# Thirty-two spare bytes between the chunks of two operand tiles

## The chip, the cores and the metric

The kernel is one program on one core of a Trainium2 chip. The metric is device time in microseconds (us) of that core. Its engines are TensorE (PE in the profile; PEld is its loading of weights), VectorE (DVE), ScalarE (ACT), GpSimd (POOL) and SyncE (SP), which issues most of the DMAs.

## The reference

Two layers of a transformer over 256 image tokens and 256 context tokens, D = 1024, all in float32. Layer 0 mixes tokens by retention (4 heads), layer 1 by attention in a neighbourhood window (32 heads). Around each mixer and each MLP stand a modulation by six vectors made from a conditioning input, a gated residual and a layer norm:

```
mod = (silu_c @ ada_w[i] + ada_b[i])[:, None, :]
sh1, sc1, g1, sh2, sc2, g2 = jnp.split(mod, 6, axis=-1)
h = x * (1.0 + sc1) + sh1
y, yc = mixer(h, hc, ...)                 # projections of h and hc, then scores, then w_o
x = layer_norm(DN_ALPHA * x + g1 * y, ln_g[i, 0], ln_b[i, 0])
h = x * (1.0 + sc2) + sh2
x = layer_norm(DN_ALPHA * x + g2 * (square(relu(h @ w1)) @ w2), ln_g[i, 1], ln_b[i, 1])
```

The context stream `hc`/`ctx` goes through the same steps in layer 0. The output is x, 256 x 1024.

## The kernel before

**Products.** Every float32 operand of a large product is split into a high and a low half (float32r tiles `hi` and `lo`; for a weight: DMA to `raw`, an ACT cast to `hi`, a DVE subtraction to `lo`). `mm3` then issues three matmuls into one PSUM bank: high x high, high x low, low x high. Each matmul first loads its stationary operand (128 columns) and then streams the moving one (512 or 256 columns); PE loads the next weights while it streams.

**The tiles of the change.** The modulated activations are kept transposed, channels on partitions, in `hTh` (high half) and `hTl` (low half): eight chunks of 128 channels, chunk k holding 512 tokens, 2048 bytes in each partition. `hs(k, a, b)` returns columns a to b of chunk k of both. They are the moving operand of the products named pq (queries and keys of retention), p (MLP hidden, from banks p1) and pn (queries and keys of layer 1), and the stationary operand of pv and pg (values and gates), pnv (values of layer 1) and p1t (four small MLP pieces). The products named p that read `hid` (second MLP matrix), pw, po, pS, pnw do not touch them.

**Where tiles lie.** Pools put tiles one behind the other. Small tiles are rounded up to 64 bytes (`LINE`, 16 floats), and every tile that a large product reads has a size that is a multiple of 512 bytes. In the built program hTh starts at byte 40,896 of each partition and hTl at 57,280, and these, all `hi`, `lo`, `raw`, `hid`, `qkh` and the rest start at 448 modulo 512. So the distance between the streamed operand of any split product and the weights that are loaded beside it is 0 modulo 512 bytes. A chunk's own start is a multiple of 64 bytes. The exceptions among PE's operands are small: `onecol` is read from byte 132 or 128 modulo 512, `cT` from 0, 128, 256 or 384, `natv` from 448, 64, 192 or 320, the identity in `cst` from 192.

**The row tile.** The modulation vectors of later stages are made in the background (`bg_stream`, L491): eight `rawa` loads are weighed and added (on DVE into `acc` or `strips`, or by matmuls), `fold_rows` sums them over partitions on PE (pada<-acc,onecol), `ada_row` (L414) adds the bias on DVE into a tile `row`, and `ada_columns` (L421) turns it by four small matmuls on PE (pada<-cst,row); parts that are gates go to DRAM instead (grow<-row). Before, `row` has a buffer of its own in the pool `smp` (one buffer of 1024 bytes), so a new row waits until the last one's readers are done. `scr` (L164) hands out one of eight buffers of 2048 bytes that all short-lived results share (`aff`, `r`, `s`, `acc`, `on`, `sg`, ...).

**What sets the order.** Code is recorded in program order and a scheduler places each engine's instructions by its own costs, except where an engine's `on` is set (then it keeps program order) and on SP. The order on each engine is fixed in the built program; engines wait for each other by semaphores. PE takes its instructions in that order, so a matmul that waits holds all behind it.

Of the kernel before, what the change touches and what calls it, by code (L numbers as in the profile page):

```python
# [10 lines left out]
F32 = mybir.dt.float32  # L11
F32R = mybir.dt.float32r
# [5 lines left out]
P = 128  # L18
D = 1024
KC = D // P  # L20
NT = 512
# [83 lines left out]
def kernel(  # L105
# [30 lines left out]
    smp = ec(tc.tile_pool(name="smp", bufs=4))  # L136
    cpool = ec(tc.tile_pool(name="cpool", bufs=1))
# [14 lines left out]
    def nm(s):  # L152
        uid[0] += 1
        return f"{s}_{uid[0]}"
# [8 lines left out]
    def scr(s, dt=F32):  # L163
        return scp.tile([P, 512], dt, tag="scr", name=nm(s))  # L164
# [248 lines left out]

    def ada_row(pr, brow, nb, p0=0, p1=P, row=None):  # L414
        if row is None:
            row = smp.tile([P, 256], F32, tag="row", name=nm("row"), bufs=1)
        dve.tensor_add(out=row[p0:p1, :nb], in0=pr[p0:p1, 0:nb], in1=brow[p0:p1, :nb])
        return row

# [50 lines left out]
    def bg_stream():  # L470
# [13 lines left out]
        for step, (l, w, part, offs, n) in enumerate(plan):  # L484
# [8 lines left out]
            if on_pe(l, w, part):  # L493
                if n == 0:
                    pr = bank("pada")
                ada_mm(pr, n, 256, lambda j: raw[:, j // 2, (j % 2) * 256 : (j % 2 + 1) * 256])
                if n == KC - 1:
                    row = ada_row(pr, brow, 256)
            elif l == 0:
                for kk in range(2):  # L500
                    for t in range(nt):
                        weigh(spare(t), raw[:, kk, :], t, 2 * (n % 4) + kk, n % 4 == 0 and kk == 0)
                if n % 4 == 3:
                    yield
                    s = n // 4
                    pr = bank("pada")
                    fold_rows(pr, (2 * s, 2 * s + 1), nt, spare)
                    row = ada_row(pr, brow, 256, 64 * s, 64 * s + 64, row)
            else:
                if n == 0:  # L510
                    acc = slot(S_VL, [P, 2, D], F32, "acc")
                for t in range(nt):

                    dve.on = n == 0 and (w, part) == (0, 0)
                    weigh(acc[:, t], raw[:].rearrange("p a n -> p (a n)"), t, n, n == 0)
                    dve.on = False
                if n == KC - 1:
                    pr = bank("pada")
                    fold_rows(pr, range(4), nt, lambda t: acc[:, t])
                    row = ada_row(pr, brow, 256)  # L520
# [32 lines left out]
        return G  # L553


    hTh = cpool.tile([P, KC, NT], F32R, tag="hTh", name="hTh")
    hTl = cpool.tile([P, KC, NT], F32R, tag="hTl", name="hTl")

    def hs(k, a, b):
        return hTh[:, k, a:b], hTl[:, k, a:b]  # L560
# [188 lines left out]
    def quarter_rows(i, raws):  # L749
        pr = bank("pada")  # L750
        for kh in range(2):
            quarter_ada(pr, raws, kh)
        return pr, ada_row(pr, brows[:, i], P)
# [33 lines left out]
    pr, row = quarter_rows(0, raws)  # L787
# [7 lines left out]
    for i in range(4):  # L795
        k = 2 * i
        quarter_q(k, 0, wq)
        if i < 3:
            pr, row = quarter_rows(i + 1, raws)
# [1073 lines left out]
```

## Time and profile before

| | |
|---|---|
| three runs | 1233.33, 1235.42, 1235.53 us; median 1235.42 |
| the profiled execution | 1232.81 us, of which the span of instructions is 1231.0 us |
| granted TensorE clock, mean | 0.994 of 2.4 GHz |
| PE busy | 1196.5 us, 97% |
| DVE, ACT, POOL busy | 809.1 (66%), 478.7 (39%), 170.7 us (14%) |
| HBM traffic | 158 GB/s over the span |

A matmul's time in the profile runs from its start to its modelled end, and neighbours overlap; what it costs a busy PE is the distance from one start to the next, called the pace below. A busy DVE costs nothing while PE has work; a chain of waits tells where it does.

### The profile page before, as it was taken

What the parts mean: (1) busy time and instruction counts of PE and PEld (TensorE: products, weight loads), DVE (VectorE), ACT (ScalarE), POOL (GpSimd) and SP (SyncE); (2) the same over time, 40 slices, a digit from 0 to 9 for tenths busy, and PEclk for the clock granted to TensorE, in tenths of its full rate; (3) what the DMA queues carried; (4) which work ended last, traced back from release to release, by engine and by line L of the source; (5) the groups of instructions that cost most, each with busy time, mean ns of one, the idle gap of its engine ahead of it and who ended that gap; (6) DMA issues with size and microseconds to landing.
All of it is one profiled execution on the core that took longest, in us unless ns stands there. A gap on an engine that the chain in (4) does not pass through costs nothing.

```text
span 1231.0 us, 17933 instructions
## 1 busy us (share of the span) xinstructions
PE 1196.5 (97%) x7069; PEld 999.1 (81%) x7069; DVE 809.1 (66%) x1256; ACT 478.7 (39%) x796; POOL 170.7 (14%) x202
## 2 busy tenths in 40 slices
PE   6999999999999999999999999999999989999996
PEld 4777888888888888888888888788787867999885
DVE  2597857777586476667666664467575678776445
ACT  2462232223223255442113342156465666565331
POOL 2004401410330140000120000131111100000002
PEclk9999999999999999999999999999999999999998
DMA  9765443375543224326656556336245543565650
GB/s 307 229 209 194 143 130 107 120 247 127 144 154 107 80 67 140 110 87 207 198 170 203 194 190 207 125 92 182 86 138 161 184 138 120 185 208 187 225 189 35
DMA packets 140660, 194.53 MB, mean 158 GB/s; under 512 B 22456, under 2 KB 84384, under 8 KB 140576
## 3 DMA queue, kind: packets, MB, share of 16 engines
q1 hardware_dynamic: 135872, 181.39, 46.2%
q0 software_dynamic: 3264, 9.46, 3.0%
q10 hardware_dynamic: 1440, 2.55, 0.6%
q8 instruction: 55, 0.90, 0.3%
q14 instruction: 29, 0.24, 0.1%
HBM read 188.53 MB, written 5.75 MB: 158 GB/s over the span
## 4 chain that ended last, share of the span: by engine, by line
PE 85%; DVE 6%; ACT 4%; DMA 2%; issue 1%; POOL 1%; DVEq 0%; SPq 0%; ACTq 0%; POOLq 0%
PE p L84 41%; PE pv L84 7%; PE pq L84 7%; PE pw L84 6%; PE pg L84 6%; PE pn L84 4%; PE pnv L84 3%; PE pada L84 2%; PE po L84 2%; ACT s L84 2%; DVE lo L84 1%; DMA rawa<-in_ada_w_dram 1%; PE ppt L84 1%; PE pS L84 1%; ACT hi L84 1%
## 5 line engine op out<-in xcount | busy, mean ns | idle before, releaser
L84 DVE TENSOR_TENSOR lo<-raw,hi 128x1024 fp32r<-128x1024 f32 (+1 forms) x227 | 278.1, 1234 | 159.4 <-ACT hi L84 158.2
L84 ACT CAST hi<-raw 128x1024 fp32r<-128x1024 f32 (+1 forms) x227 | 233.8, 1039 | 354.6 <-PE p L84 185.5
L84 PE MATMUL p<-hi,hid 128*128 128x512 f32 (+1 forms) x832 | 242.6, 374 | 0.0
L84 PEld LDWEIGHTS p<-hi,hid 128*128 128x128 f32 x832 | 152.3, 188 | 28.7 <-issue 1.2
L84 PE MATMUL p<-hTh,lo 128*128 128x256 f32 (+1 forms) x512 | 169.8, 332 | 0.8 <-DVE lo L84 0.8
L84 PE MATMUL p<-hTh,hi 128*128 128x256 f32 (+1 forms) x512 | 170.1, 333 | 0.0
L84 PE MATMUL p<-hTl,hi 128*128 128x256 f32 (+1 forms) x512 | 169.5, 331 | 0.0
L84 PE MATMUL p<-lo,hid 128*128 128x512 f32 (+1 forms) x416 | 155.5, 374 | 0.0
L84 POOL TENSOR_TENSOR R<-R,acc 128x512 f32<-128x512 f32 x40 | 65.9, 1656 | 299.0 <-DVE acc L84 298.8
L84 PEld LDWEIGHTS p<-hTh,lo 128*128 128x128 f32 x512 | 98.1, 192 | 9.8 <-DVE lo L84 1.0
L84 PEld LDWEIGHTS p<-hTh,hi 128*128 128x128 f32 x512 | 98.1, 192 | 9.5 <-issue 0.8
L84 PEld LDWEIGHTS p<-hTl,hi 128*128 128x128 f32 x512 | 98.1, 192 | 8.7
L84 DVE SCALAR_TENSOR_TENSOR acc<-rawa,scol,acc 128x1024 f32<-128x1024 f32 x49 | 62.1, 1282 | 46.7 <-DMA rawa<-in_ada_w_dram 46.6
L84 PEld LDWEIGHTS p<-lo,hid 128*128 128x128 f32 x416 | 78.4, 189 | 13.5
L84 DVE SCALAR_TENSOR_TENSOR strips<-rawa,scol,strips 128x512 f32<-128x512 f32 x84 | 69.9, 885 | 4.9 <-DMA rawa<-in_ada_w_dram 4.9
L84 ACT CAST hid<-r 128x256 fp32r<-128x256 f32 (+1 forms) x64 | 32.0, 500 | 83.5 <-DVE r L84 83.5
L84 POOL TENSOR_SCALAR rstd<-mv 128x1 f32<-128x1 f32 x28 | 9.8, 350 | 364.7 <-DVE mv L84 364.7
L84 ACT ACTIVATE s<-s,mn 128x512 f32<-128x512 f32 x64 | 45.5, 712 | 32.3 <-DVE mn L84 32.3
L84 DVE TENSOR_TENSOR hid<-r,hid 128x256 fp32r<-128x256 f32 (+1 forms) x64 | 34.6, 541 | 29.8 <-ACT hid L84 29.6
L84 PE MATMUL pq<-hTh,hi 128*128 128x512 f32 x128 | 49.9, 393 | 2.0 <-ACT hTh L84 2.0
L84 PE MATMUL pw<-hi,oh 128*128 128x512 f32 x128 | 51.3, 401 | 0.0
L84 PE MATMUL pg<-hi,hTh 128*128 128x512 f32 x128 | 51.0, 398 | 0.0
(192 smaller groups left out, 2249.5 us busy)
## 6 DMA issues: line engine op xcount, KB each, us to landing
raw<-in_mlp_w_dram SPq DMA_DIRECT2D x128, 512.0 KB
rawa<-in_ada_w_dram SPq DMA_DIRECT2D x80, 512.0 KB
raw<-in_ret_w_in_dram SPq DMA_DIRECT2D x46, 512.0 KB
raw<-in_nat_w_in_dram SPq DMA_DIRECT2D x24, 512.0 KB
rawq<-in_ada_w_dram SPq DMA_DIRECT2D x16, 512.0 KB
raw<-in_ret_w_o_dram SPq DMA_DIRECT2D x16, 512.0 KB
bias<-rpb_rows POOLq DMA_DIRECT2D x16, 256.0 KB, 4.1
raw<-in_nat_w_o_dram SPq DMA_DIRECT2D x8, 512.0 KB
```

The source lines that it names most:

```text
L84: r = f(*args, **kwargs)
```

## The change

`hTh` and `hTl` are allocated with 520 columns a chunk instead of 512 and used through a view of the first 512. Chunk k of hTh now starts at 448 + 32k modulo 512 and, since a tile is now 16,640 bytes, chunk k of hTl at 192 + 32k: sixteen different distances (0, 32, ... 480 modulo 512) to the weights, some 140 to 270 products on each. Chunks with odd k start at an odd multiple of 32 bytes. The two tiles grow by 512 bytes in sum; to make room `row` gives up its own buffer and is taken from the shared `scr` buffers. All other large tiles move down by 512 or 1024 bytes and keep 448 modulo 512. The number of instructions on every engine stays the same.

```
     def ada_row(pr, brow, nb, p0=0, p1=P, row=None):
         if row is None:
-            row = smp.tile([P, 256], F32, tag="row", name=nm("row"), bufs=1)
+            row = scr("row")[:, :256]
         dve.tensor_add(out=row[p0:p1, :nb], in0=pr[p0:p1, 0:nb], in1=brow[p0:p1, :nb])
         return row
...
-    hTh = cpool.tile([P, KC, NT], F32R, tag="hTh", name="hTh")
-    hTl = cpool.tile([P, KC, NT], F32R, tag="hTl", name="hTl")
+    hTh = cpool.tile([P, KC, NT + 8], F32R, tag="hTh", name="hTh")[:, :, :NT]
+    hTl = cpool.tile([P, KC, NT + 8], F32R, tag="hTl", name="hTl")[:, :, :NT]
```

Since `row` comes from other buffers, the scheduler places a few instructions of DVE, POOL, SP and PE otherwise, all in the background modulation beside the second half of layer 0's MLP. Two places matter below. The first is DVE at the start of the last quarter of the second MLP matrix (775 us in the trace before), where acc_6189 to acc_6198 empty four finished banks, the BN_STATS begin a layer norm, and row_6183 is a row whose turning PE waits for. Before:

```order
L84 TENSOR_TENSOR lo_6148<-raw_6145,hi_6147 128x1024
L84 TENSOR_TENSOR acc_6189<-p_935_5900,G_4624 128x512
L84 TENSOR_TENSOR acc_6192<-p_936_5901,G_4624 128x512
L84 BN_STATS st_6340<-R_110 128x6
L84 TENSOR_TENSOR acc_6195<-p_937_5902,G_4624 128x512
L84 BN_STATS st_6342<-R_110 128x6
L84 BN_STATS st_6344<-R_111 128x6
L84 TENSOR_TENSOR row_6183<-pada_6178,brow_5942 128x256
L84 TENSOR_TENSOR acc_6198<-p_938_5903,G_4624 128x512
```

There the row stands behind three of the four emptyings and three BN_STATS. On the same engine, now:

```order
L84 TENSOR_TENSOR lo_6148<-raw_6145,hi_6147 128x1024
L84 TENSOR_TENSOR row_6183<-pada_6178,brow_5942 128x256
L84 TENSOR_TENSOR acc_6189<-p_935_5900,G_4624 128x512
L84 TENSOR_SCALAR mod_109<-pada_6178 128x8 x2
L84 TENSOR_TENSOR acc_6192<-p_936_5901,G_4624 128x512
L84 TENSOR_TENSOR acc_6195<-p_937_5902,G_4624 128x512
```

The row is now the first of them, and the emptyings follow it. At two earlier places (595 and 640 us) row_4922 and row_5229 move ahead of four emptyings in the same way.

The second place is the step before it (730 us), on DVE: acc_5945 is the first weighing of the next background step. Before:

```order
L84 TENSOR_TENSOR lo_5907<-raw_5904,hi_5906 128x1024
L84 TENSOR_TENSOR row_5894<-pada_5889,brow_5644 128x256
L84 TENSOR_TENSOR lo_5913<-raw_5910,hi_5912 128x1024
L84 SCALAR_TENSOR_TENSOR r_5878<-p_922_5812,r_5878 128x512
L84 TENSOR_SCALAR mod_109<-pada_5889 128x8 x2
L84 TENSOR_SCALAR acc_5945<-rawa_5886,scol 128x1024
```

Here the row follows a weight's low half directly. Now:

```order
L84 TENSOR_TENSOR lo_5907<-raw_5904,hi_5906 128x1024
L84 TENSOR_SCALAR acc_5945<-rawa_5886,scol 128x1024
L84 TENSOR_TENSOR row_5894<-pada_5889,brow_5644 128x256
L84 SCALAR_TENSOR_TENSOR r_5878<-p_922_5812,r_5878 128x512
L84 TENSOR_SCALAR mod_109<-pada_5889 128x8 x2
L84 TENSOR_TENSOR lo_5913<-raw_5910,hi_5912 128x1024
```

The weighing has come in front of the row; on PE the row's turning, which stood behind three products of bank p_935, now stands behind six.

## Rows read from the trace of the kernel before

**Rows 1.** The page: busy time by engine; the chain that ended last, by engine.
```profile
PE 1196.5 (97%) x7069; PEld 999.1 (81%) x7069; DVE 809.1 (66%) x1256; ACT 478.7 (39%) x796; POOL 170.7 (14%) x202
...
PE 85%; DVE 6%; ACT 4%; DMA 2%; issue 1%; POOL 1%; DVEq 0%; SPq 0%; ACTq 0%; POOLq 0%
```

**Rows 2.** The chain in order of time: start us, us, what, in 140 to 215.
```profile
143.51 21.76 PE pq L84 x96
165.27 21.76 PE pv L84 x96
...
203.72 8.16 PE po L84 x36
```

**Rows 3.** Timeline of PE: first and last narrow product of one run of 24.
```profile
456.30 0.28 PE L84 MATMUL p<-hTh,hi 128*128 128x256 f32 x1
...
459.05 0.28 PE L84 MATMUL p<-hTh,lo 128*128 128x256 f32 x1
```

**Rows 4.** Windows: stretch; busy us of PE, PEld, DVE, ACT, POOL; granted clock, DMA share.
```profile
143.60:165.20 21.60, 21.60 (x97) 17.91 (x96) 19.09 (x30) 5.97 (x10) 3.94 (x2) 1.00 0.48 152
```

**Rows 5.** Groups by shape: products that read hTh (count | busy us, mean ns).
```profile
L84 PE MATMUL p<-hTh,hi 128*128 128x512 f32 x224 | 87.5, 391 | 0.0
...
L84 PE MATMUL p<-hTh,hi 128*128 128x256 f32 x288 | 82.7, 287 | 0.0
...
L84 PE MATMUL pq<-hTh,hi 128*128 128x512 f32 x128 | 49.9, 393 | 2.0 <-ACT hTh L84 2.0
...
L84 PE MATMUL pn<-hTh,hi 128*128 128x256 f32 x96 | 27.6, 287 | 0.0
...
L84 PE MATMUL pnv<-hi,hTh 128*128 128x512 f32 x64 | 25.8, 402 | 0.0
...
L84 PE MATMUL pn<-hTh,hi 128*128 128x512 f32 x48 | 19.3, 402 | 0.0
...
L84 PE MATMUL p1t<-hi,hTh 128*128 128x256 f32 x32 | 9.2, 288 | 0.0
```

**Rows 6.** Groups by shape: weight loads of 32 columns from small tiles.
```profile
L84 PEld LDWEIGHTS pav<-pt,natv 128*32 128x32 f32 x256 | 6.5, 110 | 1.3 <-issue 1.3
...
L84 PEld LDWEIGHTS pada<-strips,onecol 128*32 128x32 f32 x48 | 2.3, 109 | 3.3 <-issue 2.1
```

**Rows 7.** Timeline: transposes, and products of 32 weight columns.
```profile
898.83 0.82 PE L84 MATMUL ppt<-cst,s 128*128 128x128 f32 x6
...
899.68 1.08 PE L84 MATMUL pav<-pt,natv 128*32 128x128 f32 x32
```

**Rows 8.** Timeline of DVE: around the row of 775.88.
```profile
770.50 1.28 DVE L84 TENSOR_TENSOR acc<-p,G 128x512 f32<-128x512 f32 x2
...
775.27 0.69 DVE L84 BATCH_NORM_STATS2 st<-R 128x6 f32<-128x512 f32 x1 [0.74 <-POOL R L84]
775.88 0.41 DVE L84 TENSOR_TENSOR row<-pada,brow 128x256 f32<-128x256 f32 x1
```

**Rows 9.** Timeline of PE: the same place.
```profile
773.60 0.64 PE L84 MATMUL pada<-acc,onecol 128*32 128x256 f32 x8
...
774.75 0.39 PE L84 MATMUL p<-hi,hid 128*128 128x512 f32 x1
776.34 0.61 PE L84 MATMUL pada<-cst,row 128*128 128x8 f32 x4 [1.20 <-DVE row L84]
```

**Rows 10.** Timeline of DVE: around the row of 729.52.
```profile
729.52 0.42 DVE L84 TENSOR_TENSOR row<-pada,brow 128x256 f32<-128x256 f32 x1 [1.19 <-PE pada L84]
...
731.74 0.75 DVE L84 TENSOR_SCALAR acc<-rawa,scol 128x1024 f32<-128x1024 f32 x1
```

**Rows 11.** Timeline of PE: the same place.
```profile
728.81 0.64 PE L84 MATMUL pada<-acc,onecol 128*32 128x256 f32 x8
...
730.18 0.51 PE L84 MATMUL pada<-cst,row 128*128 128x8 f32 x4
```

**Rows 12.** The tile hTl: one DVE write's ns, min/median/max.
```profile
L84 DVE TENSOR_TENSOR hTl<-aff,hTh x24: 628/684/695, 18.3 to 1043.5; 128x512 fp32r<-128x512 f32 x24
```

## The prediction

> **What bounds the kernel now.** I read the page first: PE is busy 97% of the span, and 85% of the chain that ended last is PE [rows 1]. The other engines have slack; so a change counts where it alters the pace of PE's products or the few places where PE stands still. Second, the chain in order of time, for the pace. In it 96 products pq take 21.76 us, 96 products pv as much, and 36 products po 8.16 us: 226.7 ns each, all three times [rows 2]. pq streams the transposed activations, pv loads them as weights, po touches neither; the pace knows no difference. Third, the timeline of a run of narrow products: 23 starts from 456.30 to 459.05, 119.6 ns each, of 256 columns [rows 3]. The window over the pq piece has a granted clock of 1.00, that is 2.4 GHz [rows 4]. There 512 columns are 213.3 ns and 256 are 106.7 ns: either width pays some 13.3 ns more than its columns (226.7 - 213.3; 119.6 - 106.7 = 12.9).
>
> Of this remainder the change can take or add. The products that it touches, from the groups by shape [rows 5]: p has three forms of 224 wide and 288 narrow, pq three forms of 128, and pv and pg (not shown) the same, pn three of 48 wide and 96 narrow, pnv three of 64, p1t three of 32 narrow. Wide: 672 + 1152 + 144 + 192 = 2160. Narrow: 864 + 288 + 96 = 1248. Together 3408; 2160 x 0.2267 + 1248 x 0.120 = 639 us, 52% of the span. One ns on each is 3.4 us.
>
> **The change, part 1: the chunks.** No instruction is added. What may move is the pace at a distance other than 0 modulo 512, and at an odd multiple of 32 bytes. No split product in this trace runs at such a distance, so the cost is bounded from the nearest rows. Below: the whole remainder is a collision of load and stream and goes at fifteen of the sixteen distances, 3408 x 13.3 ns x 15/16 = -42.5 us. Above: a chunk that starts off a 64-byte boundary costs one 64-byte piece more, 16 columns or 6.7 ns, on the half that are odd: 1704 x 6.7 ns = +11.4 us.
>
> The nearest rows say nothing happens. Loads of 32 columns take 110 ns from `natv` at four residues (448, 64, 192, 320), and 109 ns from `onecol`, of which half start at 132, not even at a multiple of 8 [rows 6]. The 32 products from `natv` follow each other in 1.08 us less the last one's 0.27 us (the length of one), 0.81 us for seven and a half steps of four, 108 ns for four of 128 columns, two at a time: no delay at any of four distances [rows 7]. [...] They show that another distance doesn't hurt; they can't show whether it helps, since their streams are shorter than their loads. I take 0.
>
> [...]
>
> Writes into the chunks: 28 casts on ACT, 24 subtractions on DVE and 4 on POOL. They write 512 columns in one chunk or 128 in each of four, and one on DVE takes 628 to 695 ns over both layouts [rows 12]. No write at an odd 32 bytes is in the trace; with that spread as the price, 28 x 0.067 = 1.9 us if PE waited for every one, and as much less at the other end. I take 0: all but a few lie under products.
>
> **Part 2: the row in shared buffers.** This moves instructions, and one move meets a wait of PE. At 774.75 PE starts the third product after pada<-acc,onecol; at its pace the next would start at 774.98, but it is the turning of the row, and starts at 776.34 [rows 9]. The row was late on DVE: it ran at 775.88, behind emptyings and BN_STATS that themselves waited for POOL [rows 8], though pada had ended at 773.60 + 0.64 = 774.24. Now it follows the subtraction before 770.50 directly; DVE waits for pada, and the row is done at 774.24 + 0.41 = 774.65, 0.33 us before PE asks. So the whole wait goes: 776.34 - 774.98 = **-1.36 us**.
>
> What is late instead: four emptyings, two of which ran at 770.50 and now start at 774.65. They set free four of the eight PSUM banks. p_982, p_983, p_984 and pada have the other four; p_985 needs the first emptying (0.64 us, done by 775.3) and starts after three groups of six products, 3 x 6 x 0.2267 = 4.1 us after 774.3. The low halves of weights behind them come some 1 to 2 us later, and PE takes those four weight tiles on, 4 x 24 x 0.2267 = 21.8 us. Both are covered with us to spare. The same holds at 595 and 640 us, where PE did not wait before.
>
> At 730 us the weighing now precedes the row: pada ends at 728.81 + 0.64 = 729.45, the weighing takes 0.75 and the row 0.42 [rows 10, 11], so the row is done by 730.62. PE asked for it at 730.18 and now asks three products later, at 730.86. 0.24 us remain: cost 0. If the weighing's raw tile has not landed by 729.45 this cover goes; it had by 731.74, when it was used without a wait, so at most 2.29 - 0.24 = 2.05 us.
>
> A row now holds one of eight shared buffers, between its two halves even through much of a retention head, and its gate DMA must land before a later `acc`, `r` or `s` may have it. Such a wait would stand on DVE or ACT, with the emptyings or casts of weights queued behind it, and PE behind those; the rows' DMAs leave long before the next user stands in line, so 0.
>
> **Sum.** 1232.81 - 1.36 = 1231.45 us for the profiled execution, which was 2.61 us under the median of the three runs. On the median: 1235.42 - 1.36 = **1234.1 us**. A measurement of this kernel tells some 0.2%, 2.5 us, from no change, so this counts as within it.
>
> **Rivals.** *The remainder is a collision (faster).* Load and stream start together at distance 0 and one holds the other for 32 columns' time. For it: the remainder is equal for 512 and 256 columns, as a cost of each load would be, and the 32-column products don't show it [rows 2, 3, 7]. Against: it doesn't differ between products whose tiles lie anywhere from 40 to 220 KB, and exchanging 128 weights may cost as much by itself. If it goes at half the distances: 1234.1 - 21 = 1213; at fifteen of sixteen: 1191.5 us.
>
> [...]
>
> *Odd chunks read slower (slower).* The small tiles of this kernel are rounded up to 64 bytes, so every chunk now starts on such a boundary; afterwards half don't. If PE fetches by such pieces, an odd chunk needs one more, on the weight side above all where a narrow product leaves 10 ns beside its load: 1234.1 + 11.4 = **1245.5 us**. For it: nothing here ever ran so. Against: `onecol` [rows 6]. It decides from 2.3 ns for an odd product on (1704 x 2.3 ns = 3.9 us, which is 1.36 + 2.5).
>
> [...]
>
> *The row's wait comes back.* The buffers' waits, or the 730 place, eat the 1.36 us: 1234 to 1236, the same verdict.
>
> **How the numbers follow.** Pace unchanged, with or without the row's gain: 0.47, of which 0.39 within 0.2%, 0.05 faster and 0.03 slower. Collision: 0.31, all faster. Odd chunks: 0.22, all slower. Faster 0.36, same 0.39, slower 0.25. The forecast's own range is 1230 to 1238. For 8 in 10 I go down to the collision at half its distances, 1213, and up to the full price of odd chunks, 1246; a full collision below and a dearer misalignment above are left out, about 0.1 each.
>
> **What would show it.** Right: pq and pv still 21.76 us for 96, a narrow run still 120 ns a step, and no wait before pada<-cst,row near 775 us. Collision: pq and pv below 226 ns while po keeps 226.7. Odd chunks: products with odd k above 226.7, or narrow ones above 120, those with even k not. The part on the row is wrong if the gap at 775 us stays, or a new one stands before p_985 or near 730 us. The whole is wrong if the time leaves 1230 to 1238 while the paces stay.

## The result, and the profile after

The changed kernel takes 1240.01 us (median of 5 runs, 1239.30 to 1242.63); the kernel before took 1233.59 us beside it (5 runs, 1233.00 to 1235.53). The ratio is 1.0050, with a 95% interval of 1.0037 to 1.0063: **slower, by some 6 us**. The span of the profiled execution went from 1231.0 to 1237.6 us.

The chain of the changed kernel in order of time (start us, us, what), the lines that answer to [rows 2]:

```profile
145.25 22.30 PE pq L84 x96
167.56 22.30 PE pv L84 x96
195.67 11.11 PE pg L84 x48
206.77 8.16 PE po L84 x36
```

pq and pv have gone from 226.7 to 232.3 ns for a product. po, which touches neither hTh nor hTl, stays at 226.7. The narrow run that answers to [rows 3], in PE's timeline:

```profile
462.59 0.28 PE L84 MATMUL p<-hTh,hi 128*128 128x256 f32 x1
...
465.32 0.28 PE L84 MATMUL p<-hTh,lo 128*128 128x256 f32 x1
```

Its 23 steps take 118.7 ns each, where they took 119.6. So the wide products (512 columns) lost and the narrow ones (256 columns) gained a little. PE's timeline at the place of [rows 9], and DVE's row:

```profile
782.26 0.64 PE L84 MATMUL pada<-acc,onecol 128*32 128x256 f32 x8
...
783.40 0.39 PE L84 MATMUL p<-hi,hid 128*128 128x512 f32 x1
783.64 0.51 PE L84 MATMUL pada<-cst,row 128*128 128x8 f32 x4
```

```profile
782.97 0.42 DVE L84 TENSOR_TENSOR row<-pada,brow 128x256 f32<-128x256 f32 x1 [3.73 <-PE pada L84]
```

PE takes the turning of the row 0.24 us after the product ahead of it: the wait of [rows 9] is gone. DVE makes the row directly behind pada, as computed.

**Where the time went.** From here on a pace is the mean step from one product's start to the next one's, over all products of a kind; steps over 256.7 ns (wide: 512 columns) and over 150 ns (narrow: 256 columns), some 30 ns above the paces in [rows 2] and [rows 3], are left out as waits. "Streamed" products stream hTh or hTl, "loaded" ones load them as weights. The terms of the two profiled executions:

- wide streamed (pq, p, pn): 1170 steps, 227.0 to 232.5 ns, +6.4 us
- wide loaded (pv, pg, pnv): 914 steps, 227.6 to 232.1 ns, +4.1 us
- narrow streamed (p, pn): 1138 steps, 119.9 to 118.2 ns, -1.9 us; narrow loaded (p1t): 87 steps, 119.8 to 118.7, -0.1 us
- the row's wait: -1.36 us
- one stretch of before at half clock (0.50 granted): -1.4 us. PE had been busy 1.44 of the 3 us from 466 on. In the windows of before (columns as in [rows 4]) 17 products started in 3.4 us at 0.50, which take 17 x 0.120 = 2.0 us at full clock:

```profile
469.50:472.90 3.40, 3.40 (x17) 3.40 (x18) 3.22 (x7) 2.52 (x5) 0.00 (x0) 0.50 0.52 154
```

The windows of the changed kernel have 1.00 there (PE busy 1.73 of the 3 us ahead):

```profile
474.00:477.00 3.00, 2.25 (x18) 1.96 (x17) 2.51 (x5) 2.75 (x7) 0.00 (x0) 1.00 0.10 18
```

Together +5.7 us of the 6.6 us. Of the 0.9 us that is left, some 0.4 us would be the 76 of 2160 wide products whose steps are left out here, if they slowed like the others (an estimate); the rest is not named. Such a half-clock stretch stands in some of the profiles below (`row_only`: 0.52 at 470.8 to 474.2) and not in others of the same order of instructions (`all32`), so it is not put down to the change; what halves the clock was not shown.

### The profile page after: what moved, and what is told of

Its sections match the earlier page's. It is cut to its first block, busy times and chain, and to the rows that moved or that the text cites. A ratio compares the mean times of both kernels' runs of the same rounds, so it can differ in the third digit from the quotient of the medians.

```text
span 1237.6 us, 17937 instructions
## 1 busy us (share of the span) xinstructions
PE 1204.2 (97%) x7069; PEld 995.8 (80%) x7069; DVE 811.9 (66%) x1256; ACT 478.1 (39%) x796; POOL 173.4 (14%) x202
## 4 chain that ended last, share of the span: by engine, by line
PE 90%; DVE 4%; ACT 2%; DMA 2%; issue 1%; POOL 1%; DVEq 0%; SPq 0%; ACTq 0%; POOLq 0%
PE p L84 41%; PE pv L84 7%; PE pq L84 7%; PE pw L84 6%; PE pg L84 6%; PE pn L84 5%; PE pnv L84 4%; PE pada L84 2%; PE po L84 2%; PE ppt L84 2%; PE pS L84 1%; PE pav L84 1%; PE pqk L84 1%; DVE lo L84 1%; PE pt L84 1%; DMA rawa<-in_ada_w_dram 1%
## 5 line engine op out<-in xcount | busy, mean ns | idle before, releaser
L84 POOL TENSOR_TENSOR R<-R,acc 128x512 f32<-128x512 f32 x40 | 69.8, 1756 | 304.8 <-DVE acc L84 304.8
L84 PEld LDWEIGHTS p<-hTl,hi 128*128 128x128 f32 x512 | 96.5, 188 | 10.5 <-DVE hTl L84 0.4
L84 PE MATMUL pv<-hi,hTh 128*128 128x512 f32 x128 | 51.4, 403 | 0.0
```

Of the source, the lines that this page charges most:

```text
L84: r = f(*args, **kwargs)
```

## The experiments

"Distance" is the address of the streamed operand less that of the weights that are loaded beside it for the next product, here modulo 256 bytes (experiment 3 shows why). Theory A: the distance sets a product's pace. B: a start at an odd multiple of 32 bytes costs time (the prediction's rival). C: only a change of distance from product to product costs time. All these kernels have the row's edit and, but for `mlp64turn`, the instructions of the changed kernel in the same order on every engine.

**1. The row alone** (`row_only`).
```
-            row = smp.tile([P, 256], F32, tag="row", name=nm("row"), bufs=1)
+            row = scr("row")[:, :256]
```


> Only the row tile moves to the shared buffers; the chunks stay 2048 bytes apart, all distances 0. The order of instructions is that of the changed kernel on every engine. All three theories on the pace: pq and pv 21.76 us for 96 products (226.7 ns), narrow runs 120 ns, as before. My step on the row: no wait before pada<-cst,row near 775 us (before 1.36 us too long, changed kernel none), so 1232.2 us, 1.4 us under before. If the shared buffers cost something elsewhere: 1233 to 1236 us.

1233.41 against 1235.03 us, ratio 0.9987 (0.9977 to 0.9997): -1.6 us. The paces are those of before. PE's timeline at the place of the wait:

```profile
776.13 0.39 PE L84 MATMUL p<-hi,hid 128*128 128x512 f32 x1
776.36 0.51 PE L84 MATMUL pada<-cst,row 128*128 128x8 f32 x4
```

No wait: the row's edit is worth what the prediction said within its interval, and all of the loss is the chunks'.

**2. Odd starts at distance 0** (`all32`): every tile that a large product reads lies 32 bytes further.
```
-    RR = [cpool.tile([P, 2, D], F32, tag=f"R{t}", name=f"R{t}") for t in range(2)]
+    RR = [cpool.tile([P, 2 * D + 8 * (1 - t)], F32, tag=f"R{t}", name=f"R{t}") for t in range(2)]
+    RR = [RR[t][:, 8 * (1 - t) :].rearrange("p (a d) -> p a d", a=2) for t in range(2)]
```


> Row in shared buffers, chunks 2048 bytes apart, but hTh, hTl and every tile behind them 32 bytes further on: all distances between stream and load stay 0, all starts lie at an odd multiple of 32 bytes. Theory B (odd 32-byte starts read slower, my slower rival): pace of all wide products about 232 ns and time above 1245 us, since the products that do not read the chunks are hit too. Theories A (the distance of a product's stream to the load beside it sets its pace) and C (the change of distance from one product to the next does): 226.7 and 120 ns, 1232 us.

Ratio 0.9981 (0.9972 to 0.9991), paces 227.1 (wide streamed), 227.6 (wide loaded) and 119.9 ns (narrow streamed). Its chain:

```profile
147.38 21.76 PE pq L84 x96
169.14 21.76 PE pv L84 x96
196.71 10.88 PE pg L84 x48
```

B falls: with every start at an odd multiple of 32 bytes pq and pv keep their 226.7 ns.

**3. One distance for all** (`const64`, `const256`, then 32, 96, 128 and 192): the chunks lie close again, and both tiles are moved as a whole.
```
-    hTh = cpool.tile([P, KC, NT], F32R, tag="hTh", name="hTh")
-    hTl = cpool.tile([P, KC, NT], F32R, tag="hTl", name="hTl")
+    hTh = cpool.tile([P, KC * NT + 16], F32R, tag="hTh", name="hTh")
+    hTh = hTh[:, 16 : 16 + KC * NT].rearrange("p (k t) -> p k t", k=KC)
+    hTl = cpool.tile([P, KC * NT + 112], F32R, tag="hTl", name="hTl")
+    hTl = hTl[:, 0 : 0 + KC * NT].rearrange("p (k t) -> p k t", k=KC)
```


> Row in shared buffers, chunks 2048 bytes apart, hTh and hTl shifted together by 64 bytes: every product that streams them runs at distance 64, every one that loads them at 448, all starts at multiples of 64 bytes. Theory A: wide products off 226.7 ns (the changed kernel has 232.9 at its own distance 64 and 231.7 at 448), narrow ones about 118 to 120; time near 1240 us. Theory C: within a run of products nothing changes, so 226.7 and 120 ns, 1232 us. Theory B: 226.7 and 120 ns, 1232 us.

> As the run with 64 bytes, with a shift of 256 bytes: all products of the chunks at distance 256, starts at multiples of 64. Theory A: wide products near the 229.8 ns that the changed kernel has at its own distance 256, narrow ones 119; time 1235 to 1240 us. Theories B and C: 226.7 and 120 ns, 1232 us.

> The row's edit with every product of the transposed activations at one distance: 32 bytes where they are streamed, 224 (minus 32) of 256 where they are loaded; order of instructions unchanged. Theory 'distance sets the pace' (A): one pace for each of the two roles, other than at distance 0 (227.0 wide streamed, 227.6 wide loaded, 119.9 narrow), and near what the mixed kernel shows on average (232 wide, 118 narrow): wide between 229 and 236 ns, narrow between 112 and 120. Rival 'only a change of distance between neighbours costs' (C, already weakened by the constant 64 bytes): 227.0, 227.6 and 119.9 ns.

> As the run at 32 bytes, with 96 bytes streamed and 160 loaded. A: wide 229 to 236 ns, narrow 112 to 120, one pace in each role. If the smallest distance is the costly thing (a near miss), the wide products come out nearer to 227 than at 32 bytes.

> Distance 128 of 256 bytes in both roles. A with a repeat of 256 bytes: streamed and loaded alike, since 128 and minus 128 are one distance; both off 227, by the farthest distance that there is. If the repeat were 128 bytes the paces would be those of distance 0 (227.0, 227.6 and 119.9 ns).

> Distance 192 streamed and 64 (minus 192) loaded: the constant 64-byte run with the two roles exchanged. A with the distance alone: the paces are exchanged too, streamed wide 233.3 and narrow 116.6 ns, loaded wide 229.2 and narrow 114.6 ns. Rival 'the role decides, the sign doesn't' (D): streamed wide stays at 229.2, loaded wide at 233.3, narrow streamed at 114.6.

Measured, in ns (`const64` was profiled twice, see 6; its second values are behind a stroke). The four last ran once each, beside one run of before at 1234.24 us:

| kernel | streamed at | wide | narrow | loaded at | wide | narrow | us |
|---|---|---|---|---|---|---|---|
| row_only | 0 | 227.0 | 119.9 | 0 | 227.6 | 119.9 | ratio 0.9987 |
| const256 | 256 | 227.0 | 119.9 | 256 | 227.6 | 119.8 | ratio 0.9986 |
| const64 | 64 | 229.2 / 229.1 | 114.6 / 117.8 | 192 | 233.3 / 233.3 | 116.6 / 115.4 | ratio 1.0007 |
| const32 | 32 | 233.3 | 116.7 | 224 | 233.2 | 118.2 | 1240.73 |
| const96 | 96 | 233.3 | 120.0 | 160 | 234.0 | 118.6 | 1247.19 |
| const128 | 128 | 232.7 | 118.8 | 128 | 232.7 | 118.5 | 1244.93 |
| const192 | 192 | 233.3 | 117.0 | 64 | 230.7 | 117.3 | 1240.88 |

The chain of `const256`, then of `const64`, `const32` and `const192`:

```profile
144.05 21.76 PE pq L84 x96
165.81 21.76 PE pv L84 x96
```

```profile
145.19 22.00 PE pq L84 x96
167.19 22.39 PE pv L84 x96
```

```profile
144.97 22.40 PE pq L84 x96
167.37 22.39 PE pv L84 x96
```

```profile
144.13 22.40 PE pq L84 x96
166.53 22.39 PE pv L84 x96
194.73 10.99 PE pg L84 x48
```

At distance 256 both pieces are back at 21.76 us, so 256 bytes is as good as none (227.0 and 119.9 ns streamed at both; the change has eight distances in this sense, not sixteen). A's own numbers for the first two did not come: it expected some 229.8 ns and 1235 to 1240 us at 256 bytes, and near 1240 us at 64, where the narrow products won back most of what the wide ones lost. C falls as the only cause: at a constant 32 bytes pq (22.40 us for 96) is as slow as in the changed kernel (22.30). There the chunks start 32 bytes further on than in `row_only`, as in `all32`; only in `all32` the weights moved along, and pq kept its pace. So it is not the chunks' place by itself but their distance to the weights that counts. In `const192` the two roles have changed places with `const64`: streamed wide products went from 229.2 to the 233.3 expected, pg came down to 10.99 us for 48 (229.0 ns) as a product at 64 bytes; pv did not (233.2). So the distance decides over most of it, and the role alone doesn't; but one distance can have two paces. Why pv kept the slower one was not tested. No distance measured makes wide products faster than 0 does (227.0 and 227.6 ns); the narrow ones gain but for those at 256 and those streamed at 96 (120.0), most where streamed at 64 (114.6 for 119.9 in one execution).

The mean of the wide column over the eight distances (roles averaged where both were measured, which is at 0, 64, 128 and 192) is (227.3 + 233.3 + 230.0 + 233.3 + 232.7 + 234.0 + 233.3 + 233.2) / 8 = 232.1 ns; the changed kernel had 232.1 to 232.5. Experiment 4 asks whether such a mean is more than a coincidence.

**4. 64 bytes between chunks** (`pad64`).
```
-    hTh = cpool.tile([P, KC, NT], F32R, tag="hTh", name="hTh")
-    hTl = cpool.tile([P, KC, NT], F32R, tag="hTl", name="hTl")
+    hTh = cpool.tile([P, KC, NT + 16], F32R, tag="hTh", name="hTh")[:, :, :NT]
+    hTl = cpool.tile([P, KC, NT + 16], F32R, tag="hTl", name="hTl")[:, :, :NT]
```


> The change with 64 bytes between chunks in place of 32, and the row's edit: products at distances 0, 64, 128 and 192 of 256 in equal numbers. Theory A, that a product's time is a function of its distance alone, by the means of the constant runs: wide streamed (227.0 + 229.2 + 232.7 + 233.3) / 4 = 230.6 ns, wide loaded (227.6 + 230.7 + 232.7 + 233.3) / 4 = 231.1, narrow streamed (119.9 + 114.6 + 118.8 + 117.0) / 4 = 117.6; so 1170 x 3.6 + 915 x 3.5 - 1220 x 2.3 = +4.6 us, with the row's -1.6 some 3 us more than before, ratio 1.002 to 1.003, half of what the 32 bytes cost. Rival 'what costs is that the distance changes between neighbours, added to the distance itself': wide products at 232 ns or more as in the changed kernel, ratio 1.005 or more.

1239.60 against 1234.05 us, ratio 1.0045 (1.0029 to 1.0061); wide 231.9 streamed and 231.7 loaded, narrow 118.3. This lies between the two expectations: the table's means are 1.3, 0.6 and 0.7 ns too low. A product's time is therefore not a function of its own distance alone. The changed kernel says the same: its wide streamed products that stand at distance 0, some 140, took between 231 and 232 ns, not 227.0. Whether the neighbours' cost is carried over or the change of distance costs something by itself, beside the distance, these runs don't separate.

**5. The layer-1 MLP alone at 64 bytes** (`mlp64`): what the table offers, narrow products at 64 and wide ones at 0. The context columns are free there.
```
-        hi, lo = hTh[:, ks, tsl(t)], hTl[:, ks, tsl(t)]
+        cols = slice(16 + t * P, 16 + (t + 1) * P)
+        hi, lo = hTh[:, ks, cols], hTl[:, ks, cols]
...
+    def hs(k, a, b):
+        return hTh[:, k, 16 + a : 16 + b], hTl[:, k, 16 + a : 16 + b]
```


> The row's edit, and of the activations only those of the layer-1 MLP moved: its two token tiles are written and read 16 columns (64 bytes) further in each chunk, so that the 672 narrow streamed products p and the 96 narrow p1t run at distance 64 (minus 64 where loaded) and every wide product stays at distance 0. Theory A with the paces of the constant 64-byte run (p 114.1 ns, p1t 116.6 against 119.9 and 119.8): 672 x 5.8 ns + 96 x 3.2 ns = 4.2 us less, with the row's 1.6 us about 5.8 us less, ratio 0.9953 (0.994 to 0.997); wide products stay at 227.0 and 227.6 ns. Rival 'the stage is bound by something else' (the weights' transfers or the evacuations): the products run at 114 ns but the time comes back as waits, ratio as with the row's edit alone, 0.9987.

1230.53 against 1234.05 us, ratio 0.9966 (0.9951 to 0.9981): **faster than the kernel before** by 0.3%, of which the row's edit alone gave 0.13%, and by less than expected. In the list of PE's waits no new one of this stage stands; but the stage's long row of products p, 623 steps with no other work of PE between them, ran at 117.8 ns a step, not at 114.1 (first step, and the product behind the last):

```profile
1054.10 0.28 PE L84 MATMUL p<-hTl,hi 128*128 128x256 f32 x1
...
1127.47 0.39 PE L84 MATMUL p<-hi,hid 128*128 128x512 f32 x1
```

48 and 80 bytes gave the long row 118.3 ns each (one run each, 1233.50 and 1232.65 us), which none of the expected values is: neither a smooth curve through the table nor whole steps of 32 or 64 bytes. Between 117.8 and the 120.0 of `const96` the value at 80 bytes would fit a smooth curve; the one at 48 bytes, above both 116.7 and 117.8, would not.

> As the kernel that moves the layer-1 MLP's activations alone, by 12 columns (48 bytes). If the pace goes smoothly with the distance: between the narrow paces at 32 and 64 bytes (116.7 and 114.1 ns), some 115.4 ns. If it goes by whole steps of 32 or 64 bytes: 116.7 or 114.1.

> The same with 20 columns (80 bytes). Smooth: between 114.1 (64 bytes) and 120.0 (96 bytes), some 117 ns. Whole steps: one of the two.

**6. Two paces at one distance.** In `const64` the same 623 products, at the same distance, had run at 113.3 ns (1132.12 - 1061.51 over 623):

```profile
1061.51 0.28 PE L84 MATMUL p<-hTl,hi 128*128 128x256 f32 x1
...
1132.12 0.39 PE L84 MATMUL p<-hi,hid 128*128 128x512 f32 x1
```

Does the place of the weights decide (`mlp64pad` leaves 512 bytes free behind hTl, which gives the stage the addresses of `const64`)? Does the execution (`mlp64again` and `const64again` are `mlp64` and `const64` once more)?

> As the kernel that moves only the layer-1 MLP's activations by 64 bytes, with 512 bytes left free behind hTl, so that activations and weights of that stage lie exactly where they lay in the constant 64-byte run. Theory 'the place decides' : p at 113.3 ns, 623 x 4.4 ns = 2.7 us less than without the 512 bytes, ratio about 0.994. Rival 'how the stage begins decides' (the products before it run at other paces than in the constant run): p at 117.7 ns, ratio 0.9966 as without the 512 bytes, or either by execution.

> The kernel that moves only the layer-1 MLP's activations by 64 bytes once more, word for word. 'The place decides': p at 117.7 ns again, all 623 in a row. 'By execution': 113.3 or 117.7 ns.

> The constant 64-byte kernel once more. If what runs ahead of the stage decides: 623 products p at 113.3 ns again, wide products 229.2 streamed and 233.3 loaded. If the execution decides: 117.7 ns may come out.

`mlp64pad`: ratio 0.9965 (0.9952 to 0.9978), 117.8 ns; the place doesn't decide. `mlp64again`: 117.8 ns. `const64again`, word for word the kernel that had 113.3:

```profile
1061.35 0.28 PE L84 MATMUL p<-hTl,hi 128*128 128x256 f32 x1
...
1134.73 0.39 PE L84 MATMUL p<-hi,hid 128*128 128x512 f32 x1
```

(1134.73 - 1061.35) / 623 = 117.8 ns, and its span is 1235.2 us in place of 1232.6. So one program has two paces here, and all 623 products of an execution had the same one. The wide paces of the two executions agree to 0.1 ns. The two executions were on two different chips, so it is not shown that the execution decides and not the chip. The chip alone doesn't: on that of `const64` the 48 products ahead of the long row, at the same distance, had taken 117.9 ns each, and on that of `const64again` the next kernel shows both paces in one execution.

`mlp64turn` moves the pair of transposes pt at which the long row begins:
```
+            if f4 == 1 and f2 == 1:
+                turn_block(r11, 1, 1)
             if f4 == 1 and f2 == 0:
-                turn_block(r11, 1, 1)
```


> The layer-1 MLP's activations moved by 64 bytes, and the pair of transposes that breaks into its products stands 48 products later, so that the first row is some 96 long and the second some 575. If what stands ahead of a row of products picks one of the two paces: rows at 117.7 or at 113.3 ns, and a change from one to the other only at a break, never inside a row. At 113.3 ns in the long row: 575 x 4.4 ns = 2.5 us less than without the move, ratio 0.9945; at 117.7 ns 0.9966.

1229.09 against 1234.65 us, ratio 0.9952 (0.9937 to 0.9967). PE's timeline:

```profile
1050.00 0.28 PE L84 MATMUL p<-hTl,hi 128*128 128x256 f32 x1
...
1060.65 0.28 PE L84 MATMUL p<-hTh,lo 128*128 128x256 f32 x1
1060.77 0.38 PE L84 MATMUL pt<-cst,r 128*128 128x128 f32 x2
...
1061.71 0.28 PE L84 MATMUL p<-hTh,hi 128*128 128x256 f32 x1
...
1128.84 0.40 PE L84 MATMUL p<-hi,hid 128*128 128x512 f32 x1
```

Before the break 94 steps of 113.3 ns (10.65 / 94), behind it 570 of 117.8 (67.13 / 570). The pace changed at the break and nowhere else, as expected if a row is held by how it begins; what picks the pace stays open. The ratio of 0.9952 is the lowest measured; its interval overlaps that of `mlp64`, so the move of the transposes is not shown to help.

Last, two other distances for this stage:

> The layer-1 MLP's activations moved by 48 columns (192 bytes). By the constant run at 192 bytes p takes 117.6 ns; if two paces belong to a distance and the stage's beginning picks one, 113.3 ns may come out as well. p1t (distance 64 where loaded): 117.3 ns.

> The layer-1 MLP's activations moved by 8 columns (32 bytes). By the constant run at 32 bytes p takes 116.7 ns, p1t 118.2; another value would say that 32 bytes has more than one pace too.

One run each: at 192 bytes the long row ran at 117.8 ns and p1t at 117.8 (1231.69 us), at 32 bytes at 116.7 and 118.2 (1231.27 us). All four agree with the constant runs to 0.5 ns. But 192 bytes has a second pace too. In `const192` the 48 products ahead of the long row took 113.7 ns each over 46 steps, and the long row behind the transposes 117.8 (second and last product of the first, second of the long row, and the product behind it):

```profile
1059.52 0.28 PE L84 MATMUL p<-hTl,hi 128*128 128x256 f32 x1
...
1064.75 0.28 PE L84 MATMUL p<-hTh,lo 128*128 128x256 f32 x1
...
1065.21 0.28 PE L84 MATMUL p<-hTl,hi 128*128 128x256 f32 x1
...
1138.58 0.39 PE L84 MATMUL p<-hi,hid 128*128 128x512 f32 x1
```

At 32 bytes the mean is that of the constant run (116.7), but its steps go from 113 to 120 ns where the constant run's are 116 and 117.

## Why the prediction was wrong

The measured 1240.0 us lies above the forecast's own 1230 to 1238. The step that failed is part 1: "They show that another distance doesn't hurt; they can't show whether it helps, since their streams are shorter than their loads. I take 0." The term is +8.5 us: +10.5 on the wide products, which went from some 227 to 232 ns, and -2.0 on the narrow ones, inside the bounds of -42.5 and +11.4 that stood beside the 0. (The 213.3 and 106.7 ns behind these bounds take 2.4 columns a ns; the paces of before, 226.7 and 119.6 ns for 512 and 256 columns, make it 256 / 107.1 = 2.39.) The nearest rows [rows 6, 7] were loads of 32 columns and streams of 128; they couldn't show what 128 columns loaded beside 512 do, in either direction, and the prediction used them for one direction. (The products from `natv` that it counts as two at a time start in fours, 0.11 us from four to four: 899.82, 899.93, 900.03 us.) That pq, pv and po had one pace [rows 2] said nothing either, as all three stood at distance 0.

**Odd chunks read slower** was the only rival that forecast a slower kernel (1245.5 us), and had the sign right by luck, for its reason is false: odd starts cost nothing (227.1 ns wide and 119.9 narrow in `all32`), and wide products at 64, 128 and 192 bytes are slow too (229.2, 232.7 and 233.3 ns streamed). The sign that it named, even chunks at 226.7 ns, did not show: the even chunk at distance 0 took 231 to 232. No run shows the terms of its sum: neither the 64-byte piece of 6.7 ns, nor the 10 ns beside a narrow product's load. In the trace of before the loads of these products take 0.19 us each and start 0.12 us apart, as the products do (p<-hTh,hi from 456.53 us, p<-hTl,hi from 456.65).

**The remainder is a collision** fits narrow products in part: at 64 bytes up to 6.6 of their some 13 ns go (119.9 to 113.3), though that it is a collision which goes was not shown. For the wide ones the sign is the other way (229.2 to 234.0 ns in the table) at every distance measured but 256, where nothing moved.

That the distance costs time is plainest in two runs: 96 pq took 21.76 us at distance 0 (`all32`) and 22.40 at 32 (`const32`), with the same instructions in the same order. That load and stream meet in the memory would explain it, but was not shown; only the distance was.

**Part 2 held**, step for step: the row is done at 782.97 + 0.42 = 783.39, 0.25 us before PE turns it (0.33 forecast); the wait is gone; the edit alone measured -1.6 us (-2.8 to -0.4) where -1.36 was forecast. In the list of PE's waits of the changed kernel no row is named any more, and `row_only` has no loss; so the waits that were priced at 0 (shared buffers, the 730 us place) did not come, as far as these can show. The writes into odd chunks, taken as 0, were not measured apart, but DVE's 24 writes of hTl kept their median of 684 ns.

## What to carry to other kernels

A pace that is equal at one operand distance says nothing of another. Before operands that stream beside weight loads are moved, move them all by one constant and read the chain: one run at 64 bytes would have shown 22.0 and 22.4 us for 21.76. Here 512-column products want their streamed operand and the next weights 0 or 256 bytes apart (227.0 ns at both, 229.2 to 233.3 at the others measured), and 256-column ones gain a little at 64 (113.3 or 117.8 ns for 119.9), in stages that have only these. A single profile can be half of a story: the same kernel had two paces in one stage, in two executions.

## What was not expected of the hardware

- Products of 512 columns cost 2 to 6.4 ns more at the distances measured other than 0 and 256 bytes (229 to 234 ns against 227.0 streamed and 227.6 loaded), those of 256 columns up to 6.6 ns less (113.3 against 119.9, at 64): there the sign turns with the width.
- At one distance whole rows of products hold one of two paces: narrow ones at 64 bytes 113.3 or 117.8 ns, in two executions of one kernel and in one execution of `mlp64turn`; wide ones loaded at 64 bytes 229.0 (pg) or 233.2 (pv) in one execution. What picks the pace is open.
- Mixed distances can cost more than the mean of their constant runs: 231.9 against 230.6 ns with 64 bytes between chunks, though 232.1 to 232.5 against 232.1 with 32.
